# Where the causal mask of the diagonal is added: by products with the identity on TensorE, or by additions on VectorE

## The chip, the cores and the metric

The kernel runs on one core of a Trainium2 chip. The metric is the time of one execution on the device in microseconds (us). Runs of the kernel before took 2440.66, 2438.67 and 2438.85 us; the median is 2438.85 us. One further execution was profiled; its time was 2437.35 us, and the span that its profile shows is 2435.5 us, at a granted TensorE clock of 0.999.

## What is computed

A trunk of two layers over 2048 tokens of width 1024. Layer A normalises its input, projects it to q, k, v, forget logits and a gate, and runs causal attention with 16 heads of 64, in which the logits get a cumulated log forget gate. Layer B is a sliding-window attention over shared keys and values. The part that the change touches is layer A's attention:

```python
logits = einsum('bqhd,bkhd->bhqk', qi, k) * scale
logits = logits + ci[..., :, None] - c_k[..., None, :]
causal = k_pos[None, :] <= q_pos[:, None]
logits = where(causal, logits, -inf)
p = softmax(logits, axis=-1)
out = einsum('bhqk,bkhd->bqhd', p, v)
```

All tensors are float32.

## The kernel before, in words

Nearly all products are in float32, split into a high and a low part so that three products make one. The stages are: layer A's projections (from the start to about 590 us in the profile), layer A's attention (about 590 to 1440 us), its output projection (to about 1560 us), then layer B.

Layer A's attention (`attention_a`) goes over 64 units, 16 heads (`h`) times 4 chunks of 512 queries (`ch`). In a unit, keys are on the partitions and queries along the free dimension, so a tile of scores is 128 keys by up to 512 queries. A unit has 2 * ch + 2 steps of two key blocks each (320 steps in all, 20 per head). The steps with p < 2 * ch are full. The last two of a unit lie on the diagonal: step p = 2 * ch has blocks of 512 and 384 queries in two PSUM banks; step p = 2 * ch + 1, which the code calls `last`, has blocks of 256 and 128 queries in one bank. In each of these four blocks the first 128 queries cross the diagonal, and need the mask `mask_s` (0 or -1e30, bf16).

`scores` does one step. TensorE makes each block of scores from two products, L994 (q and k) and L995 (67 rows: the low parts, the forget rows and the row with the maximum). Then the mask comes in: on a diagonal step, one more product per block accumulates identity times mask onto the first 128 queries of the bank (L1003, 128 columns, two for each step p = 2 * ch; L999, 2 * 128 columns in one product, one for each `last` step). ScalarE takes the exponential out of PSUM (L1009, or L1000 in `last`), rounds it to the high part (L1012), GpSimd makes the low part (L1013), and VectorE adds the exponentials into an accumulator in PSUM (L1022) that L913 sums up at the end of the unit. Three steps later (`V_LAG`) `values` multiplies with v (L1037).

Beside this run two more streams. `max_pieces`, 13 steps ahead (`AHEAD`), finds the maximum of each query: a product of 66 rows into a bank of the kind `mx` (L949), and a reduction of it by VectorE (L962, or L957 with the mask of the diagonal fused in; L965 joins the parts). There are two pieces per step on average, 40 per head. `gate` feeds in the products of the gate (L1079), whose weights come by DMA (`wr`), and whose results go through VectorE (L1090, L1092) and ScalarE (L1091).

PSUM has eight banks in this stage: three for scores (`sc`), two for pieces (`mx`), one for the values (`pa`), one for the gate (`pb`), one for the accumulator (`ac`). A product into a bank waits until the last reader of that bank's former tile is done.

The order of the instructions on each engine is static. The framework makes it when the kernel is built: on each engine it takes, of what its own timing takes as ready, what stands first in the program, and sets the semaphores. `keep_in_program_order` pins an instruction behind the one written before it; L1007 pins the second mask product of a step p = 2 * ch in this way. At run time each engine works through its list in order, and an instruction that waits holds up all that stands behind it on its engine.

`constants` makes the identity in bf16 (`identb`, L243) and `mask_s` (L246) once at the start.

## Time and profile before

| | us |
|---|---|
| median of 3 runs | 2438.85 |
| profiled execution, its own time | 2437.35 |
| its span in the profile | 2435.5 |
| TensorE (PE) busy in the span | 2411.8 |
| VectorE (DVE) busy | 1729.5 |
| ScalarE (ACT) busy | 1261.4 |
| GpSimd (POOL) busy | 999.5 |

The start of a row in a timeline is measured; the end of a product on TensorE is modelled, and consecutive products overlap in the profile, so what a product costs in a packed stream is the distance from its start to the next start. PEld is the loading of weights into TensorE, which overlaps its products. A row "X <- Y: 3.0, 10, 0.4" in the table of waits says that X waited for Y for 3.0 us in all, 10 times, at most 0.4 us.

### The profile page before, as it was taken

To read this page: it belongs to the slowest core of one execution; us is meant where nothing else is said; L and a number is where in the kernel's file an instruction comes from. 1 tells how busy PE (TensorE), PEld (TensorE's weight loads), DVE (VectorE), ACT (ScalarE), POOL (GpSimd) and SP (SyncE) were. 2 spreads that over 40 slices of the span, in tenths; PEclk is the share of its full clock that TensorE was granted. 3 is DMA by queue.
4 is the path that set the end of the run, shared out by engine and by line. 5 is a ranking of instruction groups with operands and counts; after the bars stand their busy time and mean duration, and the time that the engine had idled before them with its cause. 6 is when DMAs were issued, how large, how long until landed. Compare 5 with 4: busy or idle time off the path is not lost.

```text
span 2435.5 us, 36294 instructions
## 1 busy us (share of the span) xinstructions
PE 2411.8 (99%) x11966; PEld 2028.7 (83%) x11966; DVE 1729.5 (71%) x4099; ACT 1261.4 (52%) x2504; POOL 999.5 (41%) x643
## 2 busy tenths in 40 slices
PE   9999999999999999999999999999999999999999
PEld 7888899987888788888888878888888888888887
DVE  7756567735999888888888865556766523777776
ACT  5433324323878778777877761135322312555554
POOL 0000000011878777777778852200011000477775
PEclk9999999999999999999999999999999999999999
DMA  6656545677554655575466559965433425555552
GB/s 191 205 163 195 156 149 169 195 244 234 162 166 131 204 157 146 147 211 175 131 195 173 170 143 312 298 230 160 126 101 107 139 68 163 180 179 178 178 182 74
DMA packets 351516, 419.24 MB, mean 172 GB/s; under 512 B 64928, under 2 KB 248256, under 8 KB 345152
## 3 DMA queue, kind: packets, MB, share of 16 engines
q1 hardware_dynamic: 351328, 416.92, 57.4%
q8 instruction: 95, 1.56, 0.3%
q14 instruction: 93, 0.76, 0.1%
HBM read 265.29 MB, written 151.40 MB: 171 GB/s over the span
## 4 chain that ended last, share of the span: by engine, by line
PE 89%; DVE 4%; DMA 3%; ACT 2%; POOL 1%; issue 1%; SPq 0%; DVEq 0%; ACTq 0%; POOLq 0%
PE b L775 30%; PE pa L1037 10%; PE pb L1079 7%; PE b L1260 5%; PE sc L994 5%; PE sc L995 5%; PE mx L949 5%; PE pb L1473 5%; PE pb L738 3%; PE b L738 3%; PE pa L1403 2%; PE b L1324 2%; PE pa L359 1%; PE pa L1260 1%; PE pb L359 1%
## 5 line engine op out<-in xcount | busy, mean ns | idle before, releaser
L775 PE MATMUL b<-wh,big 128*128 128x512 f32 (+3 forms) x2560 | 772.2, 375 | 3.0 <-ACT wh L502 2.4
L1013 POOL TENSOR_TENSOR big<-st,big 128x1024 fp32r<-128x1024 f32 (+1 forms) x320 | 656.0, 2070 | 242.9 <-ACT big L1012 161.3
L775 PEld LDWEIGHTS b<-wh,big 128*128 128x128 f32 x2560 | 471.4, 188 | 75.2 <-ACT wh L502 4.8
L775 PE MATMUL b<-wl,big 128*128 128x512 f32 (+3 forms) x1280 | 474.1, 371 | 0.8 <-DVE wl L503 0.8
L1022 DVE TENSOR_TENSOR ac<-ac,st 128x512 f32<-128x512 f32 (+3 forms) x576 | 352.5, 612 | 51.9 <-ACT st L1009 24.3
L1009 ACT ACTIVATE st<-sc 128x512 f32<-128x512 f32 (+1 forms) x512 | 273.7, 582 | 117.6 <-PE sc L995 48.6
L1037 PE MATMUL pa<-big 128*128 128x512 f32 (+3 forms) x1280 | 320.5, 366 | 0.6 <-POOL big L1013 0.6
L1012 ACT CAST big<-st 128x1024 fp32r<-128x1024 f32 (+1 forms) x320 | 295.2, 923 | 8.5
L775 PEld LDWEIGHTS b<-wl,big 128*128 128x128 f32 x1280 | 241.7, 189 | 35.9 <-DVE wl L503 3.5
L1037 PEld LDWEIGHTS pa<-big 128*128 128x128 f32 x1280 | 229.9, 190 | 39.2 <-POOL big L1013 2.2
L962 DVE TENSOR_REDUCE mt<-mx 128x1 f32<-128x384 f32 (+1 forms) x360 | 214.2, 598 | 29.7 <-PE mx L949 27.1
L511 ACT ACTIVATE sq<-b,r 128x512 f32<-128x512 f32 (+2 forms) x128 | 77.8, 608 | 302.8 <-PE b L775 299.8
L994 PE MATMUL sc<-big 128*128 128x512 f32 (+3 forms) x640 | 233.2, 368 | 1.1 <-DVE st L558 1.1
L995 PE MATMUL sc<-big 67*128 67x512 f32 (+3 forms) x640 | 229.4, 367 | 0.0
L949 PE MATMUL mx<-big 66*128 66x512 f32 (+2 forms) x600 | 224.7, 379 | 0.2
L1079 PE MATMUL pb<-wh,wr 128*128 128x512 f32 x488 | 178.6, 398 | 3.3 <-DMA wr<-wg 3.2
L513 DVE TENSOR_REDUCE sm<-sq 128x8 f32<-128x512 f32 (+2 forms) x128 | 74.9, 585 | 139.3 <-ACT sq L511 139.1
L875 POOL MEMSET rot<- 128x512 bf16 x1 | 0.5, 525 | 418.6 <-PE pb L359 418.6
L1372 POOL TENSOR_TENSOR big<-big,tri 128x1024 fp32r<-128x1024 f32 x60 | 143.8, 2397 | 67.1 <-DVE big L1369 62.2
L957 DVE CUSTOM_DVE_ANT_0 mx<-mx,rot 128x384 f32<-128x384 f32 (+2 forms) x240 | 146.9, 617 | 20.1 <-PE mx L949 19.3
L994 PEld LDWEIGHTS sc<-big 128*128 128x128 f32 x640 | 121.9, 190 | 23.0 <-DVE st L558 1.5
L526 POOL TENSOR_TENSOR ro<-qn,rot 128x64 f32<-128x64 f32 (+1 forms) x48 | 15.7, 328 | 298.2 <-DVE qn L517 298.2
(284 smaller groups left out, 4237.8 us busy)
## 6 DMA issues: line engine op xcount, KB each, us to landing
wr<-wg SPq DMA_DIRECT2D x62, 512.0 KB
va<-st SPq DMA_DIRECT2D x32, 512.0 KB
ka<-st SPq DMA_DIRECT2D x64, 256.0 KB
ut<-big SPq DMA_DIRECT2D x16, 1024.0 KB
big<-ka SPq DMA_DIRECT2D x16, 1024.0 KB
big<-qa SPq DMA_DIRECT2D x16, 1024.0 KB
qb<-st SPq DMA_DIRECT2D x64, 256.0 KB
big<-qb SPq DMA_DIRECT2D x16, 1024.0 KB
```

Of the source, the lines that this page charges most:

```text
L775: nc.tensor.matmul(ps[:, :n], u[tb // 4][:, dt, us], W[k][dt], start=(dt == 0 and i == 0), stop=(dt == NDT - 1 and i == 2),)
L949: mm = nc.tensor.matmul(ps, qb[:66, i * P : (i + 1) * P], kb[:66, k0:k1], start=True, stop=True,)
L957: nc.vector.tensor_tensor_reduce(out=ps, in0=ps, in1=mask_m[:, 512 - w :], scale=1.0, scalar=NEG, op0=ALU.add, op1=ALU.max, accum_out=f_(o),)
L962: nc.vector.reduce_max(o, ps, axis=AX.X)
L994: nc.tensor.matmul(o, ka[:, ks], qa[:, qs], start=not (last and n_), stop=False)
L995: nc.tensor.matmul(o, kb[:, ks], qb[:, qs], start=False, stop=not diag)
L1009: nc.scalar.activation(pf[:, off : off + w], ps[:, :w], AF.Exp, scale=HD**-0.5)
L1012: nc.scalar.copy(ph[:, :tw], pf[:, :tw])
L1013: nc.gpsimd.tensor_tensor(pl[:, :tw], pf[:, :tw], f_(ph[:, :tw]), ALU.subtract)
L1022: nc.vector.tensor_tensor(a_, a_, pf[:, off : off + w], ALU.add)
L1037: nc.tensor.matmul(pv[:, q0 : q0 + w], v[:, k, :], src[:, off : off + w], start=(p == 0 and n_ == 0 and i == 0), stop=(last and n_ == 1 an ...
L1079: nc.tensor.matmul(ps, w[:, dt // 2 % 2, wk, dt % 2, :], us[dt][uk], start=(dt == 0 and i == 0), stop=(dt == NDT - 1 and i == 2),)
```

## The change

The mask of the diagonal is no longer multiplied in. On each step p = 2 * ch VectorE adds `mask_s` onto the first 128 queries of either bank, in place in PSUM; on each `last` step one addition does both blocks (2 * 128 elements with a stride). The products L995 become the last of their accumulation. The bf16 identity and the pin of the second mask product go away.

```diff
-        self.identb = tile_("identb", [P, P], BF16)
-        nc.vector.tensor_copy(self.identb, self.ident)
...
-                nc.tensor.matmul(o, kb[:, ks], qb[:, qs], start=False, stop=not diag)
+                nc.tensor.matmul(o, kb[:, ks], qb[:, qs], start=False, stop=not last or n_ == 1)
 
             if last:
                 o = tiles[0].rearrange("p (b q) -> p b q", b=2)[:, :, :P]
-                nc.tensor.matmul(o, self.identb, self.mask_s, start=False, stop=True)
+                nc.vector.tensor_tensor(o, o, self.mask_s, ALU.add)
                 nc.scalar.activation(pf[:, :tw], tiles[0][:, :tw], AF.Exp, scale=HD**-0.5)
             else:
-                for n_, ps in enumerate(tiles if diag else ()):
-                    mm = nc.tensor.matmul(
-                        ps[:, :P], self.identb, self.mask_s[:, 0], start=False, stop=True
-                    )
-                    if n_:
-                        tc.keep_in_program_order(mm)
+                for ps in tiles if diag else ():
+                    nc.vector.tensor_tensor(ps[:, :P], ps[:, :P], self.mask_s[:, 0], ALU.add)
```

## The prediction

> **What bounds the kernel now.** I read the page first, then the busy time of layer A's attention alone, the stage of all masks, then its table of waits. The page's head:

> ```profile
> span 2435.5 us, 36294 instructions
> ## 1 busy us (share of the span) xinstructions
> PE 2411.8 (99%) x11966; PEld 2028.7 (83%) x11966; DVE 1729.5 (71%) x4099; ACT 1261.4 (52%) x2504; POOL 999.5 (41%) x643
> ```

> Busy time from 595 to 1440 us (columns: stretch, length, busy us of PE, PEld, DVE, ACT and POOL with instructions, granted clock, DMA share, GB/s), and the longest wait of PE in it for anything else:

> ```profile
> 595.00:1440.00 845.00, 840.85 (x4104) 695.26 (x4104) 736.90 (x1617) 669.28 (x1058) 667.22 (x329) 1.00 0.58 166
> ```
> ```profile
> PE pb L1079 <- DMA wr<-wg: 3.2, 3, 1.4
> ```

> TensorE is busy for 840.85 of 845 us, and what it waits for most in a whole stage is 3.2 us in three waits. So a microsecond of TensorE time that goes away is a microsecond of the kernel, as long as the other engines keep up. VectorE is the next fullest: 736.9 of 845 us, 87%, with 108 us idle. The change moves work from the one to the other.

> **What TensorE gets back.** The groups of the stage that fall away (mean ns of one behind the bar):

> ```profile
> L999 PE MATMUL sc<-mask_s,identb 128*128 128x256 bf16 x64 | 18.2, 284 | 0.0
> L1003 PE MATMUL sc<-mask_s,identb 128*128 128x128 bf16 x126 | 18.0, 225 | 0.0
> ```

> There are 64 of L999 and 128 of L1003 (two lie ahead of the stretch). Their durations would make 128 x 0.225 + 64 x 0.284 = 47 us, but products overlap; the price has to come from starts. TensorE's timeline over both diagonal steps of one unit:

> ```profile
> 1115.77 0.34 PE L995 MATMUL sc<-big 67*128 67x384 f32 x1
> 1115.95 0.29 PE L1003 MATMUL sc<-mask_s,identb 128*128 128x128 bf16 x2
> 1116.05 0.42 PE L949 MATMUL mx<-big 66*128 66x384 f32 x1
> 1116.30 1.07 PE L1037 MATMUL pa<-big 128*128 128x512 f32 x4
> ...
> 1118.08 0.22 PE L994 MATMUL sc<-big 128*128 128x128 f32 x1
> 1118.14 0.27 PE L995 MATMUL sc<-big 67*128 67x128 f32 x1
> 1118.26 0.28 PE L999 MATMUL sc<-mask_s,identb 128*128 128x256 bf16 x1
> 1118.30 0.42 PE L949 MATMUL mx<-big 66*128 66x384 f32 x1
> 1118.56 1.09 PE L1037 MATMUL pa<-big 128*128 128x512 f32 x4
> ```

> A product of 384 columns occupies 0.18 us (L995, 1115.77 to 1115.95). From that start to L1037 at 1116.30 are 0.53 us, for L995, the pair of masks and a piece of 384 columns. Without masks it would be 0.18 + 0.18 = 0.36; the pair costs 0.17 us: 0.10 of its own, and 0.07 by which the product behind it is late. In the `last` step a product of 128 columns occupies 0.06 (1118.08 to 1118.14); from 1118.14 to 1118.56 are 0.42, so the mask costs up to 0.42 - 0.06 - 0.18 = 0.18. At the low end stands the distance from its own start to the next, 0.04, if the rest of that delay belongs to the four short products in a row. I take 0.10, near the middle, since no row shows this sequence without the mask.

> Sum: 64 x 0.17 + 64 x 0.10 = 10.9 + 6.4 = 17.3 us. Ends: 64 x (0.10 + 0.04) = 9.0, and 64 x (0.17 + 0.18) = 22.4.

> [...]

> **What VectorE gets.** 128 additions of 128 elements and 64 of 256, PSUM plus a bf16 operand from SBUF. The nearest rows are its accumulator additions, and the one place where it already adds a bf16 mask onto PSUM (512 elements, layer B; its answer has min/median/max):

> ```profile
> L1022 DVE TENSOR_TENSOR ac<-ac,st 128x256 f32<-128x256 f32 x64 | 27.2, 425 | 1.8 <-ACT st L1000 0.9
> ...
> L1022 DVE TENSOR_TENSOR ac<-ac,st 128x128 f32<-128x128 f32 x64 | 18.9, 295 | 1.0
> ```
> ```profile
> L1333 DVE TENSOR_TENSOR b<-b,band x4: 689/690/690, 2057.6 to 2076.7; 128x512 f32<-128x512 f32 x4
> ```
> ```profile
> 708.34 0.42 DVE L1022 TENSOR_TENSOR ac<-ac,st 128x256 f32<-128x256 f32 x1
> 708.67 0.17 DVE L927 TENSOR_TENSOR sq<-sc,ro 64x32 f32<-64x32 f32 x1
> 708.80 0.30 DVE L1022 TENSOR_TENSOR ac<-ac,st 128x128 f32<-128x128 f32 x1
> 709.01 0.33 DVE L928 RECIPROCAL sq<-sq 64x32 f32<-64x32 f32 x1
> ```

> 295, 425 and 690 ns for 128, 256 and 512 elements lie on one line of 1.03 ns per element, so the bf16 mask costs no more than float32. In a full queue an addition of 256 holds the engine for 0.33 us (708.34 to 708.67) and one of 128 for 0.21 (708.80 to 709.01). A unit gets 2 x 0.21 + 0.33 = 0.75 us, the stage 64 x 0.75 = 48 us. By durations it would be 64 x (2 x 0.295 + 0.425) = 65 us, the upper end. VectorE then has 736.9 + 48 = 785 us of work in 845 - 17 = 828: 95%.

> **Where it would be felt.** First place, the scores: the exponential now waits for an addition that stands in VectorE's list behind what was ready earlier. I estimate 0.7 us: up to 0.3 for half an operation under way, 0.30 for the addition, 0.1 for the hop. What covers it:

> ```profile
> 1116.27 0.98 ACT L1009 ACTIVATE st<-sc 128x512 f32<-128x512 f32 x2 [1.05 <-PE sc L1003]
> ```
> ```profile
> 1120.40 0.40 PE L994 MATMUL sc<-big 128*128 128x512 f32 x1
> ```

> The two exponentials of the step at 1115 are done by 1117.25; with three banks, their banks are wanted again only behind the `last` step, from 1120.40. That is some 3 us of cover, and the values come three steps later, so I cost this at nothing; should VectorE run over 3 us late, every microsecond more is TensorE's.

> Second place, the pieces. TensorE may not start a piece before VectorE has reduced the piece two before:

> ```profile
> 1116.50 0.56 DVE L962 TENSOR_REDUCE mt<-mx 128x1 f32<-128x384 f32 x1 [0.27 <-PE mx L949]
> ```

> The piece of 1116.05 is reduced by 1117.06, and its bank is written again at 1118.30: 1.24 us to spare. Is this enough? One head by stretches: diagonal steps of its chunk 0, full steps of chunk 1, diagonal steps of chunk 1, diagonal steps of chunk 3, and the whole head:

> ```profile
> 1078.78:1084.24 5.46, 5.46 (x30) 4.32 (x29) 5.33 (x13) 3.80 (x8) 5.22 (x4) 1.00 0.47 122
> 1084.24:1089.77 5.53, 5.53 (x30) 4.79 (x29) 5.17 (x16) 5.46 (x9) 3.93 (x3) 1.00 0.73 208
> 1089.77:1094.37 4.60, 4.54 (x23) 3.50 (x22) 4.60 (x12) 4.50 (x8) 4.37 (x3) 1.00 0.67 171
> 1126.67:1131.96 5.29, 5.29 (x29) 4.35 (x28) 4.67 (x10) 5.26 (x9) 2.92 (x3) 1.00 0.77 214
> 1078.78:1131.96 53.18, 53.12 (x264) 44.14 (x263) 48.03 (x106) 41.71 (x67) 41.33 (x22) 1.00 0.58 159
> ```

> Over the head VectorE keeps room: 48.03 + 4 x 0.75 = 51.0 of 53.18 - 4 x 0.27 = 52.1 us. In the diagonal steps it doesn't. Chunk 3: 4.67 + 0.75 against 5.29 - 0.27, 0.40 us late. Chunk 0 of the next head follows at once: 5.33 + 0.75 against 5.46 - 0.27, 0.89 more. Two full steps give back 5.53 - 5.17 = 0.36. Chunk 1: 4.60 + 0.75 against 4.60 - 0.27, 1.02 more. The backlog peaks at 0.40 + 0.89 - 0.36 + 1.02 = 1.95 us, 0.71 over the 1.24 that the pieces can spare; TensorE stands for that once per head, 16 x 0.71 = 11.4 us, if its order stays as it is. The framework sets the order anew and can put other products ahead of a piece whose bank is not free, so the other end is nothing. I take 8 us, nearer to the order that the rows show.

> Lesser edits: `identb` and its copy go, once, at the start. No DMA is added or moved. The gate's weights are wanted 2% sooner; the wait of 3.2 us above may grow by a part of itself. ScalarE (669 of 845) and GpSimd (667) stay loose.

> **The sum.** 17.3 - 8 = 9.3 us off the profiled execution's 2437.35 (span 2435.5 and 1.85 around it): 2428.05. The median of the runs is 1.5 higher, 2438.85: 2429.5 us.

> **Rivals.** First: the whole saving stays, because the new order keeps the pieces out of the way. For it: PE's list is full of work that needs no VectorE (1037, 1079). Against: the 95%. It gives 2438.85 - 17.3 = 2421.5, down to 2416.5 with 22.4.

> Second: it breaks even, VectorE being at its limit. Its waits in the stage:

> ```profile
> DVE mt L962 <- PE mx L949: 27.1, 61, 1.0
> DVE ac L1022 <- ACT st L1009: 24.3, 42, 1.3
> DVE mx L957 <- PE mx L949: 19.3, 23, 2.7
> DVE ac L1022 <- ACT ac L1016: 17.4, 24, 2.4
> ```

> The waits for pieces (27.1 and 19.3) vanish when VectorE is late; those for ScalarE (24.3 + 17.4 = 41.7) needn't. If an addition holds the engine for its full duration, 736.9 + 65 + 41.7 = 843.6 us are needed, and the stage lasts as long as now: 2437.5. Against it are the starts 0.21 and 0.33 us apart. [...] The low end of TensorE's saving, 9.0 against 8 of stalls, ends in the same place.

> Third, slower: an addition that waits at the head of VectorE's list for its scores holds up the reductions behind it, TensorE reaches L949 with both banks full, and values and gate behind it stand too. Then no lateness of a diagonal stretch is carried over: 0.89 + 1.02 + 0.40 = 2.31 us per head without chunk 2, 37 in all, less 17.3: +19.7 us, 2458.5. It decides once the stalls pass 17.3 / 16 = 1.08 us per head, against the 0.5 that I take; half-way it is about 2448.

> That the change doesn't do what it says is possible in one way: the new order moves more than the masks. It has no price of its own and lies within these cases.

> **How the numbers follow.** A measurement of this kernel can tell about 0.2%, 4.9 us, from no change. Forecast, 5 to 13 us gained: 0.46. Whole saving, over 13: 0.18. Break-even, within 4.9: 0.18. Slower: 0.18. So faster 0.64, same 0.18, slower 0.18. The range runs from 2419, within the first rival, to 2447, short of the third's half-way point; some 0.05 is left out below and 0.15 above.

> **What would show it.** Right: no rows of L999 and L1003; 192 new additions of about 0.29 and 0.42 us; VectorE at 93 to 97% of the stage; the piece behind the scores at its usual 0.18; waits of PE's weight loads for L962 and L957 of 5 to 11 us; the stage about 9 us shorter, the others unchanged. Wrong: piece waits under 3 us (first rival) or over 17 (third), waits of L994 for exponentials (the cover of 3 us was too thin), or a saving of TensorE outside 9 to 22.4 us.

## The result, and the profile after

| | before | after |
|---|---|---|
| median, us | 2438.76 (4 runs, 2437.52 to 2440.66) | 2458.11 (4 runs, 2454.5 to 2459.87) |
| profiled execution, us | 2437.35 | 2454.5 |
| span in the profile, us | 2435.5 | 2452.5 |

The kernel became slower: after / before is 1.0082, 95% interval 1.0071 to 1.0094, some 20 us. The forecast was a gain of 9 us, and the range ended at 2447. In after the lines of layer A's attention stand 3 lower than in before up to L1000, and 7 lower behind: L994 and L995 are L991 and L992, the piece's product L949 is L946, the exponentials L1009 and L1000 are L1002 and L997, the low part L1013 is L1006, the accumulator L1022 is L1015, the values L1037 are L1030, the gate L1079 is L1072. The mask additions are L1000 (diagonal step) and L996 (`last`).

The head of the page, the stage from 595 to 1440 us, and the two new groups on VectorE:

```profile
span 2452.5 us, 35997 instructions
## 1 busy us (share of the span) xinstructions
PE 2409.2 (98%) x11774; PEld 2020.8 (82%) x11774; DVE 1771.3 (72%) x4290; ACT 1242.9 (51%) x2504; POOL 1001.7 (41%) x643
```
```profile
595.00:1440.00 845.00, 822.23 (x3847) 674.07 (x3846) 766.17 (x1792) 638.88 (x1041) 655.29 (x324) 1.00 0.57 164
```
```profile
L1000 DVE TENSOR_TENSOR sc<-sc,mask_s 128x128 f32<-128x128 f32 x128 | 35.5, 294 | 4.3 <-PE sc L992 4.2
L996 DVE TENSOR_TENSOR sc<-sc,mask_s 128x256 f32<-128x256 f32 x64 | 26.9, 421 | 0.6 <-PE sc L992 0.6
```

The additions take what was forecast (294 and 421 ns). TensorE, busy for 840.85 us of these 845 before, is busy for 822.23. What it waits for, in its own row and in its weight loads':

```profile
PE pa L1030 <- POOL big L1006: 16.9, 29, 1.9
PE pb L1072 <- DVE sq L1085: 2.5, 5, 0.7
```
```profile
PEld pa L1030 <- POOL big L1006: 36.4, 49, 2.3
PEld sc L991 <- ACT st L1002: 4.3, 11, 1.0
```

The wait is for GpSimd's low parts, ahead of the values. In before the same row of PE was 0.6 us, in two waits. GpSimd isn't slower (2.40 us for 1024 elements in both); it gets its input later. ScalarE's longest waits show from where:

```profile
ACT st L1002 <- DVE sc L1000: 58.9, 39, 3.4
ACT st L997 <- DVE sc L996: 50.2, 41, 2.2
```

And this is one diagonal step; its scores begin at 1099.71:

```profile
1099.71 0.39 PE L991 MATMUL sc<-big 128*128 128x512 f32 x1
1099.74 0.69 DVE L1015 TENSOR_TENSOR ac<-ac,st 128x512 f32<-128x512 f32 x1
...
1100.34 0.56 DVE L954 CUSTOM_DVE_ANT_0 mx<-mx,rot 128x384 f32<-128x384 f32 x1
1100.35 0.34 PE L992 MATMUL sc<-big 67*128 67x384 f32 x1
1100.53 0.40 PE L1030 MATMUL pa<-big 128*128 128x512 f32 x1
...
1100.81 0.73 DVE L1015 TENSOR_TENSOR ac<-ac,st 128x512 f32<-128x512 f32 x1
...
1101.45 0.29 DVE L1000 TENSOR_TENSOR sc<-sc,mask_s 128x128 f32<-128x128 f32 x1
...
1101.65 0.70 DVE L1015 TENSOR_TENSOR ac<-ac,st 128x512 f32<-128x512 f32 x1
...
1101.83 1.24 ACT L1002 ACTIVATE st<-sc 128x512 f32<-128x512 f32 x2 [0.55 <-DVE sc L1000]
...
1102.25 0.29 DVE L1000 TENSOR_TENSOR sc<-sc,mask_s 128x128 f32<-128x128 f32 x1
```

The first bank's second product is over by 1100.34; its mask is added at 1101.45, behind a piece of 0.56 us and an accumulator addition of 0.73 us that stand ahead of it in VectorE's list. Another accumulator addition stands ahead of the second mask. Over all units the median from the end of the scores to the start of the first mask addition is 1.92 us on the diagonal steps (nine in ten under 3.62) and 1.59 us in `last`. The first exponential starts 2.39 us (diagonal) and 2.32 us (`last`) after its scores; in before it was 0.52 and 0.22.

TensorE's own gain is in the same rows: L1030 starts 0.18 us behind L992 with its 384 columns, with no late product between.

Where the 20 us lie is told by an account of TensorE's starts. Each product is given what its columns occupy (0.227, 0.173, 0.119, 0.060 us for 512, 384, 256, 128; in after's stage the median distance from such a product's start to the next is 0.232, 0.177, 0.119, 0.063). Of what lies between its start and the next beyond that, 0.2 us or less is "small", and more is a stall, put to the product that comes late. The mask products and all delay ahead of them are one column. "Half clock" is the excess in stretches in which the granted clock was 0.5. The stage goes from the first product of the scores to the last of the values, in the one profiled execution (us); the products themselves need 778.6 in every row, and 782.2 where the values are pinned.

| kernel | stage | masks | values | gate | pieces | scores | half clock | small |
|---|---|---|---|---|---|---|---|---|
| before | 845.5 | 12.7 | 1.2 | 4.2 | 0.5 | 1.3 | 1.5 | 45.5 |
| after | 863.8 | 0 | 28.7 | 4.3 | 0 | 3.2 | 3.2 | 45.9 |
| no mask at all | 837.3 | 0 | 1.7 | 10.1 | 2.7 | 1.5 | 1.4 | 41.3 |
| before, load behind | 959.0 | 19.5 | 73.6 | 1.2 | 1.1 | 6.1 | 15.3 | 63.4 |
| after, masks first | 876.4 | 0 | 15.7 | 6.0 | 6.9 | 6.5 | 18.3 | 44.4 |
| after, values late | 855.3 | 0 | 9.4 | 7.9 | 1.5 | 7.8 | 5.3 | 44.9 |
| before, values late | 864.7 | 13.1 | 2.8 | 14.7 | 0.5 | 1.3 | 5.8 | 47.8 |
| after, VectorE relieved | 840.1 | 0 | 7.0 | 9.6 | 0.4 | 1.3 | 1.5 | 41.8 |
| before, tiny additions | 851.1 | 18.0 | 1.0 | 5.8 | 1.0 | 1.9 | 0 | 44.8 |
| `last` masks only | 843.4 | 7.3 | 3.4 | 6.1 | 0.5 | 1.8 | 0 | 45.9 |
| diagonal masks only | 846.4 | 5.8 | 8.4 | 5.8 | 0.3 | 1.9 | 4.3 | 41.2 |
| diagonal masks, values late | 851.2 | 5.8 | 7.0 | 12.0 | 0.2 | 1.3 | 3.0 | 43.2 |
| masks of chunks 2 and 3 | 847.9 | 6.5 | 8.4 | 6.9 | 0 | 2.0 | 1.6 | 43.9 |
| after, short low parts | 849.9 | 0 | 19.7 | 4.9 | 0 | 3.5 | 0 | 43.2 |
| after, both pinned | 877.0 | 0 | 3.5 | 19.2 | 16.1 | 3.0 | 9.2 | 43.9 |
| before, both pinned | 872.4 | 14.5 | 0.6 | 10.7 | 8.8 | 1.3 | 9.6 | 44.6 |
| after, values pinned | 867.1 | 0 | 4.2 | 16.0 | 5.7 | 9.2 | 7.6 | 42.2 |
| before, scores pinned | 867.0 | 12.9 | 14.6 | 6.4 | 0.7 | 1.8 | 4.4 | 47.8 |

Before was profiled apart from the experiments, beside which it took 2434 to 2435 us instead of 2438.8; and single executions lie up to some 6 us from the median of their kernel, in one kernel 8. So a few us between two rows' stages say nothing; the columns are read for where the time went. From before to after the stage grows by 18.3 us: -12.7 of masks, +27.5 ahead of values, +3.5 for the rest. By the same account about half of after's 28.7 us ahead of values, 14 us, stands at full steps, which have no mask: their low parts end 7.38 us (mean) after the start of their scores instead of 6.01, so the lateness spreads to the steps behind.

### The profile page after: what moved, and what is told of

It is laid out like the page before. It is cut to its first block, busy times and chain, and to the rows that moved or that the text cites. A ratio compares the mean times of both kernels' runs of the same rounds, so it can differ in the third digit from the quotient of the medians.

```text
span 2452.5 us, 35997 instructions
## 1 busy us (share of the span) xinstructions
PE 2409.2 (98%) x11774; PEld 2020.8 (82%) x11774; DVE 1771.3 (72%) x4290; ACT 1242.9 (51%) x2504; POOL 1001.7 (41%) x643
## 4 chain that ended last, share of the span: by engine, by line
PE 81%; DVE 7%; ACT 5%; DMA 3%; POOL 3%; issue 2%; SPq 0%; DVEq 0%; ACTq 0%; POOLq 0%
PE b L772 30%; PE pa L1030 8%; PE pb L1072 6%; PE b L1253 5%; PE sc L991 4%; PE sc L992 4%; PE mx L946 4%; PE pb L1466 4%; PE pb L735 3%; PE b L735 3%; ACT st L1002 1%; PE b L1317 1%; PE pa L1396 1%; DVE ac L1015 1%; POOL big L1006 1%
## 5 line engine op out<-in xcount | busy, mean ns | idle before, releaser
L1006 POOL TENSOR_TENSOR big<-st,big 128x1024 fp32r<-128x1024 f32 (+1 forms) x320 | 658.2, 2074 | 259.0 <-ACT big L1005 135.2
L1030 PE MATMUL pa<-big 128*128 128x512 f32 (+3 forms) x1280 | 350.3, 369 | 21.5 <-POOL big L1006 19.7
L1015 DVE TENSOR_TENSOR ac<-ac,st 128x512 f32<-128x512 f32 (+3 forms) x576 | 354.8, 616 | 19.4 <-ACT ac L1009 11.1
L1002 ACT ACTIVATE st<-sc 128x512 f32<-128x512 f32 (+1 forms) x512 | 286.5, 590 | 139.3 <-DVE sc L1000 59.2
L1030 PEld LDWEIGHTS pa<-big 128*128 128x128 f32 x1280 | 228.7, 190 | 79.6 <-POOL big L1006 40.4
L991 PE MATMUL sc<-big 128*128 128x512 f32 (+3 forms) x640 | 233.0, 368 | 2.4 <-ACT st L1002 1.2
L992 PE MATMUL sc<-big 67*128 67x512 f32 (+3 forms) x640 | 230.6, 368 | 0.0
L946 PE MATMUL mx<-big 66*128 66x512 f32 (+2 forms) x600 | 220.5, 370 | 0.0
L1072 PE MATMUL pb<-wh,wr 128*128 128x512 f32 x488 | 179.8, 399 | 2.6 <-DVE sq L1085 2.5
L991 PEld LDWEIGHTS sc<-big 128*128 128x128 f32 x640 | 121.9, 190 | 24.3 <-ACT st L1002 4.3
L523 POOL TENSOR_TENSOR ro<-qn,rot 128x64 f32<-128x64 f32 (+1 forms) x48 | 15.7, 326 | 298.2 <-DVE qn L514 298.2
```

What stands on the lines that cost most here:

```text
L946: mm = nc.tensor.matmul(ps, qb[:66, i * P : (i + 1) * P], kb[:66, k0:k1], start=True, stop=True,)
L991: nc.tensor.matmul(o, ka[:, ks], qa[:, qs], start=not (last and n_), stop=False)
L992: nc.tensor.matmul(o, kb[:, ks], qb[:, qs], start=False, stop=not last or n_ == 1)
L1002: nc.scalar.activation(pf[:, off : off + w], ps[:, :w], AF.Exp, scale=HD**-0.5)
L1006: nc.gpsimd.tensor_tensor(pl[:, :tw], pf[:, :tw], f_(ph[:, :tw]), ALU.subtract)
L1015: nc.vector.tensor_tensor(a_, a_, pf[:, off : off + w], ALU.add)
```

## The experiments

Sixteen kernels, in four groups; each ratio is to before on the same chip, with its 95% interval.

### The ceiling, the place and the load

**No mask at all.** Both the identity products and the additions are left out (the diff is against after):

```diff
-                nc.vector.tensor_tensor(o, o, self.mask_s, ALU.add)
-                for ps in tiles if diag else ():
-                    nc.vector.tensor_tensor(ps[:, :P], ps[:, :P], self.mask_s[:, 0], ALU.add)
-  scale=HD**-0.5
+  scale=0.01 * HD**-0.5
```

> This kernel leaves the mask of the diagonal out altogether, on either engine, and scales the exponent by a further 0.01 so that everything stays finite; all other work is the same. It measures by itself what TensorE gets back. If the prediction's first term is right, it runs 17 us under the kernel before, about 2421 (9.0 to 22.4 us under). If the term was far too large, which would be another way to explain the loss, it runs within 5 us of the kernel before, above 2434.

Measured: 2427.56 us, ratio 0.9967 (0.9957 to 0.9978). This is the ceiling for the order that the framework makes: masks at no cost on any engine bring 8 us. The account shows TensorE's term, 12.7 of masks and 45.5 - 41.3 = 4.2 of products no longer late behind them: 16.9 us. (In after "small" stays at 45.9, since more gaps of under 0.2 us come in elsewhere, behind the values' products above all: 12.0 us for 8.3.) Half of it comes back as waits, above all for the gate's weights, which are now wanted sooner than the DMA has them:

```profile
PE pb L1068 <- DMA wr<-wg: 8.4, 7, 1.9
```

**Load behind.** Before, with 192 maxima of the masks' shapes on the accumulator, behind the accumulator additions:

```diff
                 nc.vector.tensor_tensor(a_, a_, pf[:, off : off + w], ALU.add)
+            if last:
+                a_ = acc.rearrange("p (b q) -> p b q", b=4)[:, :2, :]
+                nc.vector.tensor_tensor(a_, a_, self.mask_s, ALU.max)
+            elif diag:
+                for c in (0, P):
+                    a_ = acc[:, c : c + P]
+                    nc.vector.tensor_tensor(a_, a_, self.mask_s[:, 0], ALU.max)
```

> The kernel before, with its mask products on TensorE, plus 192 VectorE instructions of the shape of the mask additions (PSUM plus the bf16 mask, 128 or 256 elements, here a maximum that changes no value), placed behind the accumulator additions of the same steps instead of ahead of the exponentials. Theory of the late exponential (the additions do harm because exponentials wait for them in VectorE's list): within 6 us of the kernel before, 2436 to 2445. Rival, VectorE's total work is the bound: the same 48 us of VectorE work without TensorE's relief costs at least as much as the changed kernel, 2458 or more.

Measured: 2550.32 us, ratio 1.0464 (1.044 to 1.0487), far over anything expected. The same work, where no exponential waits for it directly, costs 4.64%. After's 0.82% is net of TensorE's saving of some 17 us (0.7%), so this place is about three times as dear. Its stage, and the waits of PE and of ScalarE (L1044 are its values, L1013 its low parts, L1009 its exponentials):

```profile
595.00:1440.00 845.00, 788.92 (x3643) 611.00 (x3642) 703.13 (x1620) 590.36 (x931) 582.91 (x288) 0.99 0.52 151
```
```profile
PE pa L1044 <- POOL big L1013: 51.5, 72, 1.8
```
```profile
ACT st L1009 <- DVE ac L1022: 98.9, 88, 3.4
```

VectorE is busy for 703 of 845 us, 83%, a smaller share than the 87% of before: its throughput is not the bound. The exponentials wait for the accumulator additions that free the buffer `st` into which they write. So late VectorE work reaches the exponentials by two ways, the masks and the buffer, and from there the same place: values that wait for low parts, 73.6 us.

**Masks first.** After, with the additions preferred over all that is ready:

```diff
+                with tc.high_priority():
+                    nc.vector.tensor_tensor(o, o, self.mask_s, ALU.add)
```

> The changed kernel, with the mask additions given high priority when the order is made, so that they stand in VectorE's list ahead of the reductions and accumulator additions that are ready at the same time; the work is the same. Theory of the late exponential: the wait from scores to mask addition falls from 1.6 to 1.9 us (median) to about 0.5, the waits of the values for the low parts mostly go, and the time falls to 2422 to 2436. Rival, VectorE's total work is the bound: same work, same time, 2453 to 2460.

Measured: 2462.01 us, ratio 1.0113 (1.0097 to 1.0129): no gain on after, but some 0.3% more. The masks now start 0.11 us (diagonal) and 0.15 us (`last`) behind their scores (medians), but VectorE stands at the head of its list for scores that aren't there yet:

```profile
DVE sc L1002 <- PE sc L992: 34.4, 59, 2.5
```

The wait was moved, and what stood behind it in VectorE's list became late. The stalls ahead of values halve (15.7), those ahead of pieces and scores grow to 6.9 and 6.5, and 18.3 us go to stretches of half clock (last section).

**Values late.** After, with each step's values at the start of the fourth step behind it, ahead of that step's scores, and not in the middle of the third:

```diff
-V_LAG = 3
+V_LAG = 4
-            ends = len(pending) == V_LAG and closes(pending[0])
+            ends = len(pending) == V_LAG
```

> The changed kernel, with every step's values issued at the start of the fourth step after it instead of in the middle of the third (some 0.8 us more between scores and values, by two gate products and a piece); VectorE's list keeps its mask additions where they are. Theory of the late exponential: the values' waits (29 us in 44 places over 0.2 us) shrink by a third to two thirds, 2439 to 2449. Rival, VectorE's total work is the bound: no change, 2453 to 2460.

Measured: 2444.71 us, ratio 1.0045 (1.0029 to 1.006). The stalls ahead of values fall from 28.7 to 9.4 us, and by the ratios (1.0082 to 1.0045) 9 us come back. So at least 9 us of the loss are these stalls; what the later place itself costs is in its control, below.

### How much work, and where

**Tiny additions.** Before, masks on TensorE, and in addition one addition of one column per bank ahead of the exponentials of the diagonal and `last` steps (128 in all):

```diff
                 nc.tensor.matmul(o, self.identb, self.mask_s, start=False, stop=True)
+                o = tiles[0][:, :1]
+                nc.vector.tensor_tensor(o, o, self.mask_s[:, 0, P - 1 :], ALU.add)
```

> The kernel before, masks on TensorE, plus one VectorE addition of a zero onto one column of the first score bank of each diagonal step, ahead of its exponential: 128 instructions of about 0.15 us, some 13 us of work, a quarter of the mask additions, at the same place in the list. Theory of load: within 6 us of the kernel before, at most 2442. Rival, the theory of place: the exponentials wait as in the changed kernel, 2448 or more (TensorE keeps its mask products, and the stalls of 28 us before the values come on top).

Measured: 2441.08 us, ratio 1.0025 (1.0014 to 1.0037). An addition of one column takes some 0.08 us, where 0.15 was expected: from 595 to 1440 us VectorE is busy for 746.94 us with 1740 instructions, in before for 736.90 with 1617. The stalls ahead of values are 1.0 us. What ScalarE waits for VectorE, in `last` (L1001) and on the diagonal steps (L1012):

```profile
ACT st L1002 <- DVE sc L1001: 54.1, 59, 4.4
ACT st L1014 <- DVE sc L1012: 10.6, 17, 2.2
```

In `last` the exponentials do wait for VectorE, and start 1.17 us (median) behind their scores, where before has 0.22 and after 2.32. On the diagonal steps they hardly do: 0.58 us, against 0.52 and 2.39. So an operation of VectorE ahead of the exponential doesn't by itself make the loss; whether one as late as in after would, this kernel doesn't tell, since with so little work VectorE is not that late. The 0.25% lie in the mask products' column (18.0 for 12.7).

**VectorE relieved.** After, with 43 us of other VectorE work left out, the accumulator additions of the second block on diagonal and `last` steps (and the scale of the kernel without masks):

```diff
-                if p == 0 and n_ == 0:
+                if p == 0 and n_ == 0 or diag and n_:
                     continue
```

> The changed kernel with VectorE relieved of about as much as the masks cost it: on the diagonal steps the accumulator addition of the second block (384 or 128 elements) is left out, 64 x (0.46 + 0.21) = 43 us, so the sums are incomplete; the exponent is scaled by a further 0.01 to stay finite. The mask additions stand ahead of the exponentials as in the changed kernel. Theory of load (the mask additions do harm because VectorE's list loses its slack, wherever the added work stands): like the kernel without masks, 2424 to 2434. Rival, the theory of place (they do harm because the exponential must pass through VectorE's list): 2445 to 2458.

Measured: 2435.84 us, ratio 1.0006 (0.9997 to 1.0016): all of the loss is gone, but there is no gain, where 2424 to 2434 us was hoped for. What keeps it from the ceiling are the values, 7.0 us against 1.7 without masks, and the gate takes its share as there (9.6 and 10.1):

```profile
PE pb L1072 <- DMA wr<-wg: 7.4, 8, 2.5
PE pa L1030 <- POOL big L1006: 5.2, 7, 0.9
```

**The masks of `last` only, and of the diagonal steps only.** 21 and 27 us of VectorE work instead of 48; the other step's masks stay on TensorE:

```diff
             if last:
-                nc.tensor.matmul(o, self.identb, self.mask_s, start=False, stop=True)
+                nc.vector.tensor_tensor(o, o, self.mask_s, ALU.add)
```
```diff
-                for n_, ps in enumerate(tiles if diag else ()):
-                    mm = nc.tensor.matmul(
...
+                for ps in tiles if diag else ():
+                    nc.vector.tensor_tensor(ps[:, :P], ps[:, :P], self.mask_s[:, 0], ALU.add)
```

> Only the masks of the last step of a unit go to VectorE (64 additions of 256, 64 x 0.33 = 21 us); those of the step before stay products on TensorE, which gets back 64 x 0.10 = 6 us. Theory of load: 21 us fit into VectorE's slack of 108 us better than 48, so less than half of the changed kernel's loss, 2432 to 2442. Rival, the theory of place: about a third to a half of the stalls, less a third of the saving, 2440 to 2448.

> Only the masks of the step before the last go to VectorE (128 additions of 128, 64 x 0.42 = 27 us); that of the last step stays on TensorE, which gets back 64 x 0.17 = 11 us. Theory of load: 2430 to 2442. Rival, the theory of place: half to two thirds of the stalls, less two thirds of the saving, 2442 to 2450.

Measured: 2436.38 us, ratio 1.0006 (0.9997 to 1.0016), and 2433.0 us, ratio 0.9992 (0.9982 to 1.0001). Neither loses, neither gains. The account prices each step's masks on TensorE. In `last` it is (12.7 - 7.3) / 64 = 0.084 us. On the diagonal step it is (12.7 - 5.8 + 45.5 - 41.2) / 64 = 0.175 us, the 4.3 us of "small" being the products that were late behind the pair, 0.067 each. As that is a difference of two executions, here it is from before alone: from the product behind a pair to the next start lie 0.087 us (median) beyond its columns, behind other products 0.005, so some 0.08. The rows of PE, first of `last` only, then of the diagonal only, have the waits in their order:

```profile
PE pb L1079 <- DMA wr<-wg: 4.2, 7, 0.9
PE pa L1037 <- POOL big L1013: 2.1, 5, 0.6
```
```profile
PE pa L1033 <- POOL big L1009: 6.4, 8, 1.6
PE pb L1075 <- DMA wr<-wg: 5.0, 4, 3.1
```

The loss is not linear in the work: by these executions 21 us cost some 2 us of stalls ahead of values, 27 us cost 7, 48 us cost 27.5.

### Which way the lateness takes

**Short low parts.** After, GpSimd making half the columns of the low part on diagonal and `last` steps:

```diff
-            nc.gpsimd.tensor_tensor(pl[:, :tw], pf[:, :tw], f_(ph[:, :tw]), ALU.subtract)
+            pw = tw // 2 if diag and n > 7 else tw
+            nc.gpsimd.tensor_tensor(pl[:, :pw], pf[:, :pw], f_(ph[:, :pw]), ALU.subtract)
```

> After, but from the ninth step on GpSimd forms the low part for the first half of the columns only on the steps that touch the diagonal (448 of 896 and 192 of 384); the other half keeps what an earlier step left, so this part of the computation is left out. VectorE's list is that of after, masks ahead of the exponentials included. Theory of the narrow chain: VectorE's lateness costs only because GpSimd, nearly full, carries it into the following steps; freed of about 90 us, GpSimd catches up, the waits of L1030 for GpSimd fall from 60 us (PE and PEld together) under 15, and the time is 2433 to 2445 against 2434.5 for before. Theory of VectorE's load: the lateness costs by whichever way it reaches TensorE; waits for exponentials or accumulators take the place of those for GpSimd, and the time stays at 2450 to 2460.

Measured: 2442.17 us, ratio 1.0031 (1.0019 to 1.0042). The time is in the first theory's range, but its reason is not borne out: the waits were to fall under 15 us.

```profile
PE pa L1031 <- POOL big L1007: 11.5, 21, 1.1
```
```profile
PEld pa L1031 <- POOL big L1007: 23.7, 30, 1.6
```

The mean slack, from the end of a low part to the start of its first product, rises where the low part itself got shorter (diagonal 0.71 to 1.55 us, `last` 1.29 to 1.62), but in the full steps behind it stays as it was (1.51 and 1.48). Of the stalls ahead of values, those on masked steps fall from 15 to 3 us, while those on full steps stay (14 and 17). GpSimd carries next to nothing from step to step; that part of the theory has fallen. In after the second exponential of a full step ends 3.01 us behind the start of its scores, in before 2.14: the lateness is there already on ScalarE.

**Before, values late: the control.** The edit of values late, on before:

```diff
-V_LAG = 3
+V_LAG = 4
-            ends = len(pending) == V_LAG and closes(pending[0])
+            ends = len(pending) == V_LAG
```

> Before, masks on TensorE, with the values one step later in the same way as in the kernel with late values. It is the control for that kernel (1.0045 of before). In before the low parts are ready 3 to 4 us ahead of their products, so later values can bring nothing: 2432 to 2437, ratio 0.999 to 1.001, if the later place has no price of its own; then all of the 0.45% that was left over in the kernel with late values is VectorE's doing. If the later place has a price (the gate's and the scores' waits, 8 us each in that kernel), before pays it too: 2439 to 2446, and the masks then cost next to nothing once the values are late.

Measured: 2450.27 us, ratio 1.0063 (1.005 to 1.0075). The later place has a price of its own, most of it in waits for the gate's weights:

```profile
PE pb L1079 <- DMA wr<-wg: 12.4, 8, 2.5
```

So the 0.45% left over with values late is no more than that price: once the values are late, masks on VectorE cost no more than on TensorE.

**Diagonal masks, values late.** Both edits together, as a candidate for a gain:

```diff
-V_LAG = 3
+V_LAG = 4
...
-                nc.tensor.matmul(o, kb[:, ks], qb[:, qs], start=False, stop=not diag)
+                nc.tensor.matmul(o, kb[:, ks], qb[:, qs], start=False, stop=not last)
```

> The kernel with only the diagonal step's masks on VectorE (0.9992 of before), with the values one step later. Theory of the narrow chain: its 8.4 us of waits ahead of values fall away and the stage gives them back: 2425 to 2431, ratio 0.996 to 0.9985. If later values have a price of their own, or if VectorE's load costs by another way: 2433 to 2442.

Measured: 2436.61 us, ratio 1.0009 (1.0 to 1.0018). The values' stalls hardly fall (8.4 to 7.0), the gate's double (5.8 to 12.0), in an execution 6.5 us above the median. No gain.

**Masks of chunks 2 and 3 only.** 24 us of VectorE work, away from the dense run of diagonal steps in chunks 0 and 1:

```diff
+                if ch > 1:
+                    nc.vector.tensor_tensor(o, o, self.mask_s, ALU.add)
+                else:
+                    nc.tensor.matmul(o, self.identb, self.mask_s, start=False, stop=True)
```

> Before, with both steps' masks on VectorE in chunks 2 and 3 alone (24 us of VectorE work of the 48, 32 units of 64), where four or six full steps follow or precede the diagonal ones; chunks 0 and 1 keep the products with the identity. TensorE's saving is half, 8.5 us. If the lateness that runs from chunk 3 through chunk 0 into chunk 1 made the loss, it is broken here: 2427 to 2432, ratio 0.997 to 0.999. If the loss follows the amount of work on VectorE alone, it comes out as the kernels with 21 and 27 us did: 2433 to 2437, ratio 0.999 to 1.001.

Measured: 2437.6 us, ratio 1.001 (1.0001 to 1.0019), as the other halves, and 8.4 us ahead of values. It doesn't matter which half; a lateness carried from chunk 3 into chunks 0 and 1, on which the prediction's stall rested, isn't what decides.

### The order on TensorE

In the traces the slack of a low part on the diagonal step falls from 3.31 us (mean) to 0.71. The exponential's start moved from 1.27 to 3.10 us after the start of its scores: 1.83. And the values start sooner: their first product came 8.84 us after the start of the scores, and comes after 7.49. Some 0.3 of this 1.35 us is the mask products' own time, the rest a change of TensorE's list: between the two stand 44.3 products (8.2 us by their columns) in before, of which 40.6 (7.9) are not masks, 40.7 (8.0) in the kernel without any masks, and 35.1 (6.9) in after. With VectorE fuller, the framework put values ahead of scores that used to stand ahead of them. The kernel with load behind has much the same order (7.0 us, 6.8 without its mask products); relieved (7.9) and the half kernels are near before. Four kernels pin products to the order of the program; counts of the expectations are of the built lists, without the mask products of `last`.

**Both pinned, on after, and on before as the control:**

```diff
-                nc.tensor.matmul(o, ka[:, ks], qa[:, qs], start=not (last and n_), stop=False)
+                mm = nc.tensor.matmul(o, ka[:, ks], qa[:, qs], start=not (last and n_), stop=False)
+                if not n_:
+                    tc.keep_in_program_order(mm)
...
-                    nc.tensor.matmul(
+                    mm = nc.tensor.matmul(
                         pv[:, q0 : q0 + w], v[:, k, :], src[:, off : off + w],
...
+                    if not (n_ or i):
+                        self.tc.keep_in_program_order(mm)
```

> After, with the first product of each step's scores and the first of each step's values pinned in program order on TensorE. In after the framework put values ahead of the next scores: between a diagonal step's scores and its values stand 34.8 products (6.9 us by their columns), in before 42.8 (8.1 us); pinned there stand 41.8 (8.3 us), and 8.3 us in the full steps (after 7.8, before 8.3). Theory of order: half or more of the low parts' lost slack was this order, so the stalls ahead of values fall from 28.7 us under 10, and with TensorE's saving of some 17 us the time is 2426 to 2438 against 2435 for before. Theory of the late exponential alone: the masks still wait some 1.9 us behind VectorE's list, the slack stays under 2 us, the stalls ahead of values stay over 15 us, and the time is 2442 to 2455.

> Before, masks on TensorE, with the same two pins: the control. Between scores and values stand 42.9 products on the diagonal step (8.1 us) and 41.9 in the full ones (8.35 us), as without pins. Both theories: 2432 to 2438, ratio 0.999 to 1.001. If the pins have a price of their own, it shows here, and the kernel after with pins has to be set against this one.

Measured: 2468.77 us, ratio 1.0144 (1.0127 to 1.0161), and 2460.47 us, ratio 1.0106 (1.009 to 1.0121). The expected time fails: pins are dear by themselves, 1.06%. Against the control the masks on VectorE cost 8.3 us. The expected stalls are there: 3.5 us ahead of values instead of 28.7, and a mean slack of 3.31 us on the diagonal step, as in before. Even the masks' wait falls, to 0.62 us (median) on the diagonal step. What took its place, from the waits of PE and of its weight loads:

```profile
PE pb L1076 <- DMA wr<-wg: 12.0, 6, 3.0
...
PE mx L946 <- DVE mt L959: 3.2, 8, 0.7
```
```profile
PEld mx L946 <- DVE mt L954: 8.7, 20, 1.0
PEld mx L946 <- DVE mt L959: 8.5, 16, 1.2
```

These are the pieces that wait for VectorE, the second place of the prediction: 16.1 us, 7.3 more than in the control (some 1 us of the difference is a DMA). The gate has 8.5 us more.

**Values pinned, on after.** Only the second half of that edit:

```diff
+                    if not (n_ or i):
+                        self.tc.keep_in_program_order(mm)
```

> After, with only the values pinned: between scores and values stand 45.6 products on the diagonal step (9.0 us), 40.0 in the last (7.8) and 45.6 in the full ones (9.3), more than in before. Theory of order: the stalls ahead of values go under 5 us, and the time is 2426 to 2438; if the longer distance has the price that later values had in before (0.6%), 2438 to 2450 with waits for the gate's weights and no stalls ahead of values. Theory of the late exponential alone: stalls ahead of values over 10 us, 2442 to 2455.

Measured: 2455.0 us, ratio 1.0087 (1.0072 to 1.0102). The stalls ahead of values are gone here as well (4.2), and 16.0 us of gate, 9.2 of scores and 7.6 of half clock stand in their place. The sign of the theory of order is there, its time is not.

**Scores pinned, on before.** Only the first half, with the masks on TensorE:

```diff
+                if not n_:
+                    tc.keep_in_program_order(mm)
```

> Before, masks on TensorE, with only the scores pinned: the order is moved part of the way to that of after, 7.5 us between scores and values on the diagonal step, 6.7 in the last and 7.5 in the full ones (before 8.1, 7.1, 8.3; after 6.9, 6.2, 7.8), while the masks cost VectorE nothing. The low parts had 3.2 to 4.0 us of slack and lose 0.4 to 0.8 of it. If the order does harm only together with late exponentials: 2432 to 2439, ratio 0.999 to 1.0015, stalls ahead of values under 5 us. If the order by itself makes the loss: over 2441, with stalls ahead of values over 8 us.

Measured: 2457.52 us, ratio 1.0098 (1.0083 to 1.0113). With VectorE's work and the exponentials as in before, the order alone brings the wait of after (L1039 are its values, L1015 its low parts) and 14.6 us of stalls ahead of values:

```profile
PE pa L1039 <- POOL big L1015: 10.8, 13, 2.0
```

## Why the prediction was wrong

**TensorE's saving: right.** 17.3 us were forecast; 16.9 went in the kernel without masks. By steps it was 0.17 and 0.10 forecast, 0.175 and 0.084 measured, and the late product, 0.07 forecast, is 0.07 to 0.08. The masks alone measured 12.7.

**VectorE's work: right in size, wrong in its use.** The work in the stage rose by 44 us, forecast at 48, to 779 us in 863, which is 90% for the forecast 95%, as the stage grew. The durations were right, and so was the start of the next operation, forecast at 0.21 us behind an addition of 128 elements: it is 0.20 (1101.45 to 1101.65). But "95%" was treated as a stock of idle time that runs out. The kernel with load behind loses 4.6% at 83%. Who waits for an operation waits also for what stands ahead of it in its engine's list: in after the mask of 1101.45 started behind 0.56 and 0.73 us of other VectorE work, 1.11 us after its scores were over.

**The failed step: "First place, the scores".** It says that the wait is 0.7 us, and "the values come three steps later, so I cost this at nothing". The wait was composed of half an operation under way, as if the addition were next in VectorE's list; measured from the end of the scores to the start of the addition are 1.92 and 1.59 us (medians; the hop from an addition's end to its exponential, estimated at 0.1 us, has a median of 0.033), because more stands ahead: between the end of the scores and the addition VectorE starts two other operations of 0.4 us or more on the diagonal step and three in `last` (medians). The cover was read as 3 us from TensorE's wish for the scores' banks. What matters was the slack of the low parts, 3.1 to 3.8 us in the mean, and on the diagonal step it was drawn on from both sides: 1.8 us by the later exponentials, some 1.1 by the new order. The full steps behind, to which the prediction gave no wait at all, lost 1.6 us of theirs (3.10 to 1.51), and half of the stalls stand there. 28.7 us of stalls came out where nothing was costed. The prediction had listed "waits of L994 for exponentials" as the sign of a thin cover; the sign came one station later, at the values.

**The second place, the pieces: wrong for this order.** 8 us were forecast. In after no stall of over 0.2 us stands ahead of a piece, presumably because VectorE catches up with the pieces while the values wait. With the order pinned the stall exists, 7.3 us more than in the control. The text had said that the framework could set the order anew, and drew from it only a way to less ("the other end is nothing"), never a new wait.

**The rivals.** The third, slower, gave 2458.5 us, and 2458.11 were measured. That is chance: its mechanism, full banks of pieces, is not in after. The first, the whole saving, is excluded by the kernel without masks: with no mask work on any engine 8 of 17 us come through, because the gate's weights are the next to be late. The break-even, with VectorE held for the full duration of each addition, is excluded by the starts (1101.45 to 1101.65) and by the measured time. A wait for the gate's weights was foreseen ("may grow by a part of itself") and put at nothing.

**Shown and not shown.** Shown: the loss is time in which the values wait for low parts. These stalls shrink with less work on VectorE, with later values and with a pinned order. The time came back in full only with less work on VectorE; later values brought about half of it back, and with pins other stalls took the place. On before, pinned scores alone bring 14.6 us of such stalls, half of after's. Why the framework chose this order is only argued: if it reckons the scores' three banks free later, because the exponentials behind VectorE are later, values are what is ready. The shares of lateness and order in after's 28.7 us can't be parted cleanly, since pins also shortened the masks' wait. No version beat before; the nearest is the diagonal masks only, within the interval of no change.

## What to carry to other kernels

Before moving work to an engine with room, measure the ceiling by leaving the work out; here it was 0.33%, and none of the kernels that kept the work came near it. Price the moved operation where it stands: count what lies ahead of it in the list of its engine, follow the result to the product that needs it, and compare with that product's slack. And where a framework orders the instructions anew, compare the lists of the two builds between producer and consumer: a fuller engine can shorten the distance on another one.

## What the runs showed of the hardware

In some stretches of these runs TensorE's granted clock was 0.50. One such stretch of masks first (columns as in the prediction):

```profile
930.88:934.29 3.41, 3.41 (x20) 2.79 (x18) 2.38 (x7) 2.11 (x4) 2.37 (x1) 1.00 0.68 194
934.29:937.70 3.41, 2.40 (x10) 1.28 (x8) 3.40 (x12) 3.38 (x7) 2.89 (x2) 1.00 0.83 270
937.70:941.11 3.41, 3.41 (x9) 2.64 (x9) 3.41 (x8) 2.25 (x4) 1.93 (x2) 0.50 0.12 5
941.11:944.52 3.41, 3.41 (x17) 2.88 (x17) 2.75 (x7) 0.65 (x2) 2.97 (x2) 1.00 0.43 116
```
